# Second feed-forward product of a transformer block by seven half-size block products, a quarter of the depth at a time, two of them kept in PSUM

## The chip, the cores and the metric

The program runs on one core of a Trainium2 chip. The metric is the time on the device in microseconds (us), from the start of the execution to its end. The kernel before took 733.24 us, the median of three runs (732.91 to 734.58).

## The reference

One block of an encoder over 512 rows of width 1024: two attention branches, a gated mix, a layer norm, a feed-forward layer with a squared ReLU, and a second layer norm. Weights and rows are float32. What follows the two branches is

```python
x = layer_norm(DEEPNORM_ALPHA * x + mix, ln1_g[l], ln1_b[l])

h = jnp.square(jax.nn.relu(jnp.einsum("bsd,df->bsf", x, w_ff1[l])))
ff = jnp.einsum("bsf,fd->bsd", h, w_ff2[l])
x = layer_norm(DEEPNORM_ALPHA * x + ff, ln2_g[l], ln2_b[l])
```

Here `w_ff1` is 1024 x 4096 and `w_ff2` is 4096 x 1024. The first product contracts over 1024, the second over 4096; both have 512 rows.

## The kernel before

**Products of split operands.** TensorE multiplies in a reduced float32 format, so each operand is kept as two parts: a rounded one (h) and the rest (l). `split` (L82 to L87) makes them: ScalarE's cast (L84) writes h, VectorE's subtraction (L85) writes l. One product of a 128x128 block by a 128x512 block is then three matmuls, h by h, h by l and l by h: `tmm` where the weights are the stationary operand (L184 to L186), `smm` where the rows are (L189 to L191).

**The feed-forward layer** runs in two halves of the hidden width (`hf`, 2048 columns each). In a half:

- First product: eight calls of `t_pair`, each with two PSUM banks of hidden units (128 units by 512 rows), 8 depth blocks x 3 matmuls per bank. `evac_h` takes a bank out: maximum with zero on VectorE (L850), the square on VectorE (L851), then a split. The results stay in SBUF, transposed, units in partitions, and are the stationary operand of the second product.
- Second product: for each half of the output columns (`nh`) one `s_group`, four banks (128 rows by 512 columns), 16 depth blocks x 3 matmuls per bank. VectorE adds a finished bank to the residual rows `x1`. In the very last group the fourth row block is cut into two pieces of 256 columns (`cut_last`), each row block's second layer norm follows its bank, and the rows are stored.

The very first pair of banks is cut into columns 0 to 255 and 256 to 511, so that it can begin before the last row block of the first layer norm is transposed.

**Weights.** `w` is one stream of chunks, 128 x 1024 (512 KB) each. `chunk` and `prefetch` load a chunk on SP's queue (L126) into one of three `raw` buffers and split it, double-width, into one of three `wh` and `wl` buffers. A cast thus waits until TensorE has read the buffer's old chunk.

**The order.** A tile scheduler takes the program's order, with few exceptions, as the order of each engine's queue, and puts a wait on each instruction that needs another engine's result or a free buffer. In the first half, the first layer norm's scaling of the residual rows (`affine`, L742 and L748, four instructions for each of four row blocks) stands behind the pairs 1 to 4.

**SBUF and PSUM.** SBUF tiles of 128 x 512 come from rings named X (16), G (16) and V (24); PSUM has eight banks, "mm" (4), "st" (3) and "o" (1), taken in turn by `mm_bank`.

## Time and profile before

| | |
|---|---|
| median of three runs | 733.24 us |
| the profiled execution | 734.16 us, of it 732.3 us are the span |
| mean granted TensorE clock | 0.996 |
| TensorE / VectorE / ScalarE busy | 98% / 60% / 41% of the span |
| first product, first half (from its second pair on) | 385.6 to 461.7 us |
| second product, first half | 461.7 to 548.8 us |
| first product, second half | 548.8 to 635.8 us |
| second product, second half | 635.8 to 723.6 us |
| last addition starts; span ends | 723.75; 732.3 us |

In the rows, PE is TensorE, PEld its weight loads, DVE VectorE, ACT ScalarE, POOL GpSimd, SP the engine whose queue holds most DMA issues. Times are us from the span's start. In a timeline row come start, duration, engine, line, operation, output <- input, shape; in brackets the idle time of that engine before the instruction and what ended it. Instructions of one engine overlap at their ends: the distance between two starts is shorter than one duration. In a table by stretch each engine has its busy time and, in parentheses, the instructions. Of a busy share over the whole span, ask first in which stretch it arises.

### The profile page before, as it was taken

What the parts mean: (1) busy time and instruction counts of PE and PEld (TensorE: products, weight loads), DVE (VectorE), ACT (ScalarE), POOL (GpSimd) and SP (SyncE); (2) the same over time, 40 slices, a digit from 0 to 9 for tenths busy, and PEclk for the clock granted to TensorE, in tenths of its full rate; (3) what the DMA queues carried; (4) which work ended last, traced back from release to release, by engine and by line L of the source; (5) the groups of instructions that cost most, each with busy time, mean ns of one, the idle gap of its engine ahead of it and who ended that gap; (6) DMA issues with size and microseconds to landing.
All of it is one profiled execution on the core that took longest, in us unless ns stands there. A gap on an engine that the chain in (4) does not pass through costs nothing.

```text
span 732.3 us, 9147 instructions
## 1 busy us (share of the span) xinstructions
PE 720.5 (98%) x3391; PEld 602.2 (82%) x3391; DVE 437.6 (60%) x780; ACT 298.3 (41%) x506; POOL 100.5 (14%) x107
## 2 busy tenths in 40 slices
PE   9999999999999999999999999999999999999995
PEld 7888888888888888888898888888888888888884
DVE  6667668766667666745877885423235655523555
ACT  5556566645667755324353322212112332322200
POOL 2022266730121120051000000000000000000001
PEclk9999999999999999999999999999999999999998
DMA  8554223331431213464113223232232223322302
GB/s 295 199 155 134 74 84 91 99 117 58 128 102 60 85 59 115 151 225 171 58 59 115 87 86 116 87 115 87 91 111 87 96 83 110 102 100 87 115 30 86
DMA packets 27596, 78.86 MB, mean 108 GB/s; under 512 B 4640, under 2 KB 5408, under 8 KB 27552
## 3 DMA queue, kind: packets, MB, share of 16 engines
q1 hardware_dynamic: 26688, 77.17, 32.2%
q10 hardware_dynamic: 864, 1.11, 0.4%
q8 instruction: 26, 0.43, 0.2%
q14 instruction: 18, 0.15, 0.1%
HBM read 71.45 MB, written 2.10 MB: 100 GB/s over the span
## 4 chain that ended last, share of the span: by engine, by line
PE 95%; ACT 2%; DVE 2%; DMA 0%; issue 0%; DVEq 0%
PE mm L184 13%; PE mm L186 13%; PE mm L185 13%; PE mm L189 7%; PE mm L191 7%; PE mm L190 7%; PE st L191 4%; PE st L190 4%; PE st L189 4%; PE st L186 3%; PE st L185 3%; PE st L184 3%; PE o L191 2%; PE o L190 1%; PE o L189 1%; PE st L278 1%
## 5 line engine op out<-in xcount | busy, mean ns | idle before, releaser
L85 DVE TENSOR_TENSOR wl<-raw,wh 128x1024 fp32r<-128x1024 f32 (+1 forms) x116 | 141.7, 1222 | 120.8 <-ACT wh L84 120.8
L84 ACT CAST wh<-raw 128x1024 fp32r<-128x1024 f32 (+1 forms) x116 | 120.2, 1036 | 195.9 <-PE st L191 65.8
L184 PE MATMUL mm<-X,wh 128*128 128x512 f32 x256 | 103.2, 403 | 0.0
L186 PE MATMUL mm<-X,wl 128*128 128x512 f32 x256 | 99.9, 390 | 0.0
L185 PE MATMUL mm<-X,wh 128*128 128x512 f32 x256 | 99.8, 390 | 0.0
L186 PEld LDWEIGHTS mm<-X,wl 128*128 128x128 f32 x256 | 48.0, 188 | 10.6
L184 PEld LDWEIGHTS mm<-X,wh 128*128 128x128 f32 x256 | 48.1, 188 | 8.8
L185 PEld LDWEIGHTS mm<-X,wh 128*128 128x128 f32 x256 | 48.2, 188 | 8.6
L773 POOL TENSOR_SCALAR s<-s 128x1 f32<-128x1 f32 x1 | 0.4, 412 | 388.2 <-DVE s L757 388.2
L189 PE MATMUL mm<-wh,X 128*128 128x512 f32 (+1 forms) x128 | 51.0, 400 | 0.6 <-ACT wh L84 0.6
L287 ACT ACTIVATE e<-e,s 128x128 f32<-128x128 f32 (+3 forms) x64 | 36.0, 563 | 35.4 <-DVE s L285 34.6
L190 PE MATMUL mm<-wl,X 128*128 128x512 f32 (+1 forms) x128 | 50.3, 393 | 0.0
L191 PE MATMUL mm<-wh,X 128*128 128x512 f32 (+1 forms) x128 | 50.3, 393 | 0.0
L184 PE MATMUL mm<-x1t_h,wh 128*128 128x512 f32 x128 | 49.8, 389 | 0.0
L185 PE MATMUL mm<-x1t_l,wh 128*128 128x512 f32 x128 | 49.8, 389 | 0.0
L186 PE MATMUL mm<-x1t_h,wl 128*128 128x512 f32 x128 | 49.8, 389 | 0.0
L380 POOL TENSOR_SCALAR e<-e,s 128x128 f32<-128x128 f32 (+3 forms) x32 | 36.8, 1149 | 65.9 <-DVE s L289 62.0
L84 ACT CAST V<-lt 128x512 fp32r<-128x512 f32 x24 | 14.9, 620 | 62.8 <-DVE lt L851 62.8
L186 PE MATMUL st<-x1t_h,wl 128*128 128x512 f32 (+1 forms) x104 | 38.8, 373 | 0.0
L185 PE MATMUL st<-x1t_l,wh 128*128 128x512 f32 (+1 forms) x104 | 38.7, 373 | 0.0
L184 PE MATMUL st<-x1t_h,wh 128*128 128x512 f32 (+1 forms) x104 | 38.5, 374 | 0.0
L566 POOL TENSOR_SCALAR e<-e,s 128x128 f32<-128x128 f32 (+3 forms) x16 | 19.1, 1196 | 93.2 <-DVE s L565 67.8
(259 smaller groups left out, 1532.8 us busy)
## 6 DMA issues: line engine op xcount, KB each, us to landing
raw<-in_w_dram SPq DMA_DIRECT2D x118, 512.0 KB
q<-q SPq DMA_DIRECT2D x32, 128.0 KB
G<-in_relb_dram SPq DMA_DIRECT2D x8, 256.0 KB
x<-in_x_dram SPq DMA_DIRECT2D x4, 512.0 KB
...
```

Source lines behind the costliest of these rows:

```text
L84: A.copy(out=h, in_=src)
L85: i = (eng or V).tensor_tensor(out=l, in0=src, in1=h.bitcast(F32), op=ALU.subtract)
L184: T.matmul(ps, lw_h, rh, start=first, stop=False)
L185: T.matmul(ps, lw_h, rl, start=False, stop=False)
L186: T.matmul(ps, lw_l, rh, start=False, stop=last)
L189: T.matmul(ps, ah, w_h, start=first, stop=False)
L190: T.matmul(ps, ah, w_l, start=False, stop=False)
L191: T.matmul(ps, al, w_h, start=False, stop=last)
L278: T.matmul(ps[:, :n], q2[:, sl], k1[:, :n], start=False, stop=True)
L287: A.activation(e[:, :n], e[:, :n], AF.Exp, bias=nm, scale=-1.0, accum_out=sums)
L380: G.tensor_scalar(ex[:, :n], ex[:, :n], r, None, op0=ALU.mult)
L566: G.tensor_scalar(e2[:, :n], e2[:, :n], r2l, None, op0=ALU.mult)
```

## The change

The second product becomes Strassen's scheme (Winograd's form), a quarter of the hidden width (1024) at a time. In a quarter the hidden rows A (512 x 1024) and the weights B (1024 x 1024) are seen as 2 x 2 blocks, and seven products of sums of blocks replace eight products of blocks. Of A, rows 0 to 255 and 256 to 511 and the two halves of the quarter's depth are the blocks; of B, the halves of the depth and of the columns. A block product is 2 row blocks x 4 depth blocks x 3 matmuls.

- **Quarters.** The layer runs in four quarters: four pairs of the first product (the pair i makes depth block i of A's left and of its right half), then the seven products. In quarter 0 the first layer norm's scaling stands behind pair 1 (two row blocks) and pair 2 (two).
- **Left operands.** `square` has the ReLU on ScalarE and the square on VectorE. `first` and `second` form the sums of A's blocks at half width (256 rows) and split them.
- **Right operands.** Each depth block of `w2` is loaded as four 128 x 512 tiles on SP's queue. `prepare(n, i)` splits the operand of product n, and forms differences in place ahead of later ones. The lower right block is overwritten and loaded a second time for product 3, behind product 5's split. Splits are single-width.
- **Products.** The order is 1, 6, 2, 7, 5, 4, 3. Products 7 and 5 (`W`, `Z`) stay in four "mm" banks over all four quarters; the others go through the four remaining banks. The sum of products 1 and 6 over the quarters stands in SBUF (`U`), and products 1, 2, 4 and 3 are added to the residual rows `x1` in each quarter.
- **The last quarter.** `U`, `W` and `Z` are added to the residual rows, and products 7, 5, 4, 3 run by row block, so that layer norms and stores follow row block by row block (2, 0, 1, 3). The last product is cut into two pieces of 256 columns, as before.

The core of the diff:

```diff
-    def s_group(act_h, act_l, evac, before=None, nk=4, tail=1, cut_last=False, ahead=2):
+    def s_group(act_h, act_l, evac, before=None, nk=4, tail=1, ahead=2):
 
         jobs = [(s, 0, S) for s in range(NT)]
-        if cut_last:
-            jobs[-1:] = [(NT - 1, 0, S // 2), (NT - 1, S // 2, S)]
...
-    rotation[:] = ["o", "st", "st", "st", "mm", "mm", "mm", "mm"]
+    rotation[:] = ["o", "st", "st", "st"]
...
-        def evac_h(ps):
-            r = tmp_tile()
-            V.tensor_scalar(r, ps, 0.0, None, op0=ALU.max)
-            V.tensor_tensor(out=r, in0=r, in1=r, op=ALU.mult)
-            big_h = vt if len(hh) < 12 else (lambda: xt(FR))
-            h, l = big_h(), big_h()
-            split(r, h, l)
-            hh.append(h)
-            hl.append(l)
...
+    lnc1 = [[xt() for _ in range(2)] for _ in range(2)]
+    load_ln(ln1_g, ln1_b, lnc1)
...
+    U = [late.tile([P, S], F32, name=f"u{b}") for b in range(2)]
+    touched = set()
+
+    def add_to(s, nh, ps, lo=0, hi=S):
+        y = x1[s][:, nh * S + lo:nh * S + hi]
+        if (s, nh) in touched:
+            V.tensor_tensor(out=y, in0=y, in1=ps, op=ALU.add)
+        else:
+            V.scalar_tensor_tensor(out=y, in0=y, scalar=ALPHA, in1=ps, op0=ALU.mult, op1=ALU.add)
+            touched.add((s, nh))
...
+    def sub(out, a, b):
+        V.tensor_tensor(out=out, in0=a, in1=b, op=ALU.subtract)
...
+    LEFT = {1: "A11", 2: "A12", 3: "S4", 4: "A22", 5: "S1", 6: "S2", 7: "S3"}
+    lo_rows, hi_rows = slice(0, 256), slice(256, S)
...
+            a11 = self.halves(vt)
+            self.ops[1] = [(vt(), vt()) for _ in range(4)]
+            s2 = self.halves(vt)
+            self.ops[6] = [(vt(), vt()) for _ in range(4)]
+            s3 = self.halves(lambda: late.tile([P, S], FR, tag="s3", bufs=4, name=name("s3")))
...
+        def halves(self, make):
+
+            two = [(make(), make()) for _ in range(2)]
+            return [tuple(t[:, 256 * j:256 * (j + 1)] for t in pair)
+                    for pair in two for j in range(2)]
...
+        def square(self, ps):
+            t = tmp_tile()
+            A.activation(t, ps, AF.Relu)
+            V.tensor_tensor(out=t, in0=t, in1=t, op=ALU.mult)
+            return t
+
+        def first(self, i):
+            def f(ps):
+                t = self.t0 = self.square(ps)
+                sub(t[:, hi_rows], t[:, lo_rows], t[:, hi_rows])
+                split(t[:, lo_rows], *self.a["A11", i])
+                split(t[:, hi_rows], *self.a["S3", i])
+            return f
...
+        def second(self, i):
+            def f(ps):
+                t, t0 = self.square(ps), self.t0
+                s2 = tmp_tile()[:, lo_rows]
+                sub(s2, t[:, hi_rows], t0[:, hi_rows])
+                for left, right in (("A12", "A22"), ("S4", "S1")):
+                    h, l = gt(FR), gt(FR)
+                    split(t, h, l)
+                    self.a[left, i] = h[:, lo_rows], l[:, lo_rows]
+                    self.a[right, i] = h[:, hi_rows], l[:, hi_rows]
+                    if left == "A12":
+                        split(s2, *self.a["S2", i])
+                        sub(t[:, lo_rows], t[:, lo_rows], s2)
+                        V.tensor_tensor(out=t[:, hi_rows], in0=s2, in1=t0[:, lo_rows], op=ALU.add)
+            return f
...
+        def loads(self, i):
+            self.raw[i] = [self.load(i, r, c) for r, c in ((0, 0), (0, 1), (1, 1), (1, 0))]
+
+        def prepare(self, n, i, parts=None):
+            b11, b12, b22, b21 = self.raw[i]
+            src = {1: b11, 6: b22, 2: b21, 7: b12, 5: b11, 4: b22, 3: b11}[n]
+            if n == 6:
+                sub(b22, b22, b11)
+            self.ops[n][i] = self.ops[n][i] or parts or (vt(), vt())
+            split(src, *self.ops[n][i])
+            if n == 1:
+                sub(b11, b12, b11)
+                sub(b12, b22, b12)
+            if n == 6:
+                sub(b22, b21, b22)
+            if n == 5:
+                self.load(i, 1, 1, b11)
+
+        def run(self, n, ps, blocks=(0, 1), first=True, stop=True, cuts=((0, S),)):
+            jobs = [(b, lo, hi) for b in blocks for lo, hi in cuts]
+            order = [(j, i) for i in range(4) for j in jobs] if n == 1 else                 [(j, i) for j in jobs for i in range(4)]
+            for (b, lo, hi), i in order:
+                ah, al = (t[:, b * P:(b + 1) * P] for t in self.a[LEFT[n], i])
+                wh, wl = (t[:, lo:hi] for t in self.ops[n][i])
+                smm(ps[b][:, lo:hi], ah, al, wh, wl, first and i == 0, stop and i == 3)
...
+    for q in range(4):
+        qt, last = Quarter(q), q == 3
+        for i in range(4):
+            for n in ((0,), (1, 2), (3,), ())[i] if q else (i,):
+                qt.loads(n)
...
-                for _ in t_pair(*zip(*(x1t(k) for k in range(KD))), [evac_h, evac_h]):
+                for _ in t_pair(*zip(*(x1t(k) for k in range(KD))), evacs):
...
+            if q == 0 and i in (1, 2):
+                for s in (2, 3) if i == 1 else (0, 1):
+                    affine(s, *norm.pop(s), *lnc1)
+            for n, k in ((), ((1, 0),), ((1, 1), (6, 0)), ((1, 2), (1, 3), (6, 1)))[i]:
+                qt.prepare(n, k)
+
+        def prepare(n, which=range(4), parts=None):
+            for i in which:
+                qt.prepare(n, i, parts and [t[:, i, :] for t in parts])
...
+        if last:
+            t, p3h, p3l = (late.tile([P, 4, S], dt, tag="x1t", bufs=4, name=name("x1t"))
+                           for dt in (F32, FR, FR))
+            lnc = [[t[:, 2 * i + j, :] for j in range(2)] for i in range(2)]
+            load_ln(ln2_g, ln2_b, lnc)
...
+        if q == 0:
+            W, Z = ([bank("mm") for _ in range(2)] for _ in range(2))
+        ends = dict(first=q == 0, stop=last)
+        X = bank_pair()
+        qt.run(1, X)
+        prepare(6, (2, 3))
+        for b in range(2):
+            if q == 0:
+                A.copy(out=U[b], in_=X[b])
             else:
+                V.tensor_tensor(out=U[b], in0=U[b], in1=X[b], op=ALU.add)
+            add_to(b, 0, X[b])
+        prepare(2)
+        X = bank_pair()
+        qt.run(6, X)
+        prepare(7)
+        for b in range(2):
+            V.tensor_tensor(out=U[b], in0=U[b], in1=X[b], op=ALU.add)
+        X = bank_pair()
+        qt.run(2, X)
+        prepare(5)
+        for b in range(2):
+            add_to(b, 0, X[b])
             if last:
+                row_stats(b, 0)
+        if not last:
+            qt.run(7, W, **ends)
+            prepare(4)
+            qt.run(5, Z, **ends)
+            prepare(3)
+            X = bank_pair()
+            qt.run(4, X)
+            prefetch(next_chunk[0] + 4, next_chunk[0] + 2)
+            for b in range(2):
+                add_to(b + 2, 0, X[b])
+            X = bank_pair()
+            qt.run(3, X)
+            for b in range(2):
+                add_to(b, 1, X[b])
+            continue
+
+        prepare(4)
+        prepare(3, parts=(p3h, p3l))
+        for b in range(2):
+            for s, nh in ((b + 2, 1), (b + 2, 0), (b, 1)):
+                add_to(s, nh, U[b])
+        qt.run(7, W, (0,), **ends)
+        add_to(2, 1, W[0])
+        add_to(2, 0, W[0])
+        qt.run(5, Z, (0,), **ends)
+        add_to(2, 1, Z[0])
+        row_stats(2, 1)
+        X, Y = bank_pair(), bank_pair()
+        qt.run(4, X, (0,))
+        add_to(2, 0, X[0])
+        row_stats(2, 0)
+        layer_norm(2, *lnc, store_row(2))
+        add_to(0, 1, Z[0])
+        qt.run(3, Y, (0,))
+        add_to(0, 1, Y[0])
+        row_stats(0, 1)
+        layer_norm(0, *lnc, store_row(0))
+        qt.run(5, Z, (1,), **ends)
+        add_to(1, 1, Z[1])
+        add_to(3, 1, Z[1])
+        qt.run(3, Y, (1,))
+        add_to(1, 1, Y[1])
+        row_stats(1, 1)
+        layer_norm(1, *lnc, store_row(1))
+        qt.run(7, W, (1,), **ends)
+        add_to(3, 0, W[1])
+        add_to(3, 1, W[1])
+        row_stats(3, 1)
+        for lo, hi in ((0, 256), (256, S)):
+            qt.run(4, X, (1,), cuts=((lo, hi),))
+            add_to(3, 0, X[1][:, lo:hi], lo, hi)
+            row_stats(3, 0, lo, hi)
+        layer_norm_last(3, *lnc, store_row(3))
...
-    for hf in range(2):
-        for fp in range(8):
-            c = 2048 * hf + 256 * fp
-            parts.append(t_form(w_ff1[:, c:c + P], w_ff1[:, c + P:c + 2 * P]))
-        for nh in range(2):
-            parts.append(s_form(w_ff2[2048 * hf:2048 * hf + 2048, 512 * nh:512 * nh + 512]))
+    for q in range(4):
+        for i in range(4):
+            c = 1024 * q + P * i
+            parts.append(t_form(w_ff1[:, c:c + P], w_ff1[:, c + 512:c + 512 + P]))
...
+        "w2": a["w_ff2"][0].reshape(4, 2, 4, P, D).transpose(0, 2, 1, 3, 4),
```

How the order moves. The names are the pools' tiles with running numbers: `lt` hidden units before their split, `o`, `st` and `mm` PSUM banks, `wl`, `wh` and `raw` weight chunks of the first product, `x1_` the residual rows, `bn` statistics. In the new kernel X holds a quarter's raw weight blocks and V and G operands; L866 there is `sub`, L897 the square, L896 the ReLU, L853 `add_to`, L85 still the split.

VectorE, the end of the first product. Before, the last pair of the first half:

```order
L850 TENSOR_SCALAR lt982_4422<-mm981_4397 128x512
L851 TENSOR_TENSOR lt982_4422<-lt982_4422 128x512
L85 TENSOR_TENSOR wl990_4438<-raw985_4429,wh989_4437 128x1024
L85 TENSOR_TENSOR X984_4426<-lt982_4422,X983_4425 128x512
L850 TENSOR_SCALAR lt992_4466<-mm991_4441 128x512
L851 TENSOR_TENSOR lt992_4466<-lt992_4466 128x512
L85 TENSOR_TENSOR X994_4470<-lt992_4466,X993_4469 128x512
L85 TENSOR_TENSOR wl1005_4512<-raw988_4435,wh1004_4511 128x1024
L850 TENSOR_SCALAR lt996_4498<-mm995_4473 128x512
L851 TENSOR_TENSOR lt996_4498<-lt996_4498 128x512
L85 TENSOR_TENSOR wl1008_4542<-raw1003_4509,wh1007_4541 128x1024
L85 TENSOR_TENSOR X998_4502<-lt996_4498,X997_4501 128x512
```

The same place at the end of quarter 1's last pair, in the new kernel:

```order
L897 TENSOR_TENSOR lt1143_5016<-lt1143_5016 128x512
L866 TENSOR_TENSOR X1115_4843<-X1116_4845,X1115_4843 128x512
L866 TENSOR_TENSOR lt1144_5019<-lt1143_5016,lt1141_4983 128x256
L85 TENSOR_TENSOR G1146_5022<-lt1143_5016,G1145_5021 128x512
L85 TENSOR_TENSOR V1064_4636<-lt1144_5019,V1063_4635 128x256
L866 TENSOR_TENSOR lt1143_5016<-lt1143_5016,lt1144_5019 128x256
L921 TENSOR_TENSOR lt1143_5016<-lt1144_5019,lt1141_4983 128x256
L866 TENSOR_TENSOR X1116_4845<-X1117_4847,X1116_4845 128x512
L866 TENSOR_TENSOR X1094_4740<-X1094_4740,X1092_4736 128x512
L85 TENSOR_TENSOR G1148_5030<-lt1143_5016,G1147_5029 128x512
L866 TENSOR_TENSOR X1098_4748<-X1098_4748,X1096_4744 128x512
L85 TENSOR_TENSOR V1068_4640<-X1094_4740,V1067_4639 128x512
```

The maximum is gone from VectorE; between the square and the next pieces of the pair stand differences and splits of the right operands.

ScalarE at the same place, before:

```order
L84 CAST X983_4425<-lt982_4422 128x512
L84 CAST X993_4469<-lt992_4466 128x512
L84 CAST wh1004_4511<-raw988_4435 128x1024
L84 CAST wh1007_4541<-raw1003_4509 128x1024
L84 CAST X997_4501<-lt996_4498 128x512
L84 CAST wh1010_4571<-raw1006_4539 128x1024
L84 CAST wh1013_4601<-raw1009_4569 128x1024
L84 CAST wh1016_4631<-raw1012_4599 128x1024
```

ScalarE in the new kernel, at the end of quarter 1's last pair:

```order
L84 CAST wh1199_5301<-raw1137_4952 128x1024
L84 CAST V1059_4631<-X1115_4843 128x512
L84 CAST V1051_4623<-lt1141_4983 128x256
L84 CAST s31075_4647<-lt1141_4983 128x256
L84 CAST wh1235_5371<-raw1197_5297 128x1024
L896 ACTIVATE lt1143_5016<-st1142_4991 128x512
L84 CAST G1145_5021<-lt1143_5016 128x512
L84 CAST V1063_4635<-lt1144_5019 128x256
```

The last pair's first instruction on ScalarE is now the ReLU, with a weight cast (for a chunk of the next first product) directly ahead of it; before, it was the cast of the squared units.

VectorE at the end of the program, before:

```order
L888 TENSOR_TENSOR x1_2_3208<-x1_2_3208,mm1209_5876 128x512
L894 BN_STATS bn1197_5854<-x1_2_3208 128x6
L734 BN_AGGR s1234_6129<-bn1197_5854 128x2
L742 SCALAR_TENSOR_TENSOR x1_2_3208<-x1_2_3208,s1234_6129,G807_3405 128x512
L747 RECIPROCAL s1236_6131<-s1235_6130 128x1
L742 SCALAR_TENSOR_TENSOR x1_2_3208<-x1_2_3208,s1234_6129,G808_3406 128x512
L748 SCALAR_TENSOR_TENSOR x1_2_3208<-x1_2_3208,s1236_6131,G809_3407 128x512
L748 SCALAR_TENSOR_TENSOR x1_2_3208<-x1_2_3208,s1236_6131,G810_3408 128x512
L888 TENSOR_TENSOR x1_3_3209<-x1_3_3209,mm1210_5877 128x256
L894 BN_STATS bn1198_5863<-x1_3_3209 128x6
L888 TENSOR_TENSOR x1_3_3209<-x1_3_3209,o1211_5878 128x256
L894 BN_STATS bn1198_5863<-x1_3_3209 128x6
```

VectorE at the same place in the new kernel:

```order
L853 TENSOR_TENSOR x1_3_3213<-x1_3_3213,mm992_4328 128x512
L736 SCALAR_TENSOR_TENSOR x1_0_3210<-x1_0_3210,s1504_6726,x1t1453_6465 128x512
L741 RECIPROCAL s1506_6728<-s1505_6727 128x1
L736 SCALAR_TENSOR_TENSOR x1_0_3210<-x1_0_3210,s1504_6726,x1t1453_6465 128x512
L742 SCALAR_TENSOR_TENSOR x1_0_3210<-x1_0_3210,s1506_6728,x1t1453_6465 128x512 x2
L863 BN_STATS bn1487_6620<-x1_1_3211 128x6
L853 TENSOR_TENSOR x1_3_3213<-x1_3_3213,mm992_4328 128x512
L728 BN_AGGR s1507_6766<-bn1487_6620 128x2
L853 TENSOR_TENSOR x1_3_3213<-x1_3_3213,st1498_6682 128x256
L736 SCALAR_TENSOR_TENSOR x1_1_3211<-x1_1_3211,s1507_6766,x1t1453_6465 128x512
L741 RECIPROCAL s1509_6768<-s1508_6767 128x1
```

In the new kernel a row half of `x1` gets several additions, of `mm` (products 7 and 5) and `st` banks, where it got one, and additions of row block 3 stand between the instructions of row block 0's and 1's layer norms.

## Rows read from the trace of the kernel before

**Rows 1.** Part 1 of the page: busy us, share of the span, instructions
```profile
PE 720.5 (98%) x3391; PEld 602.2 (82%) x3391; DVE 437.6 (60%) x780; ACT 298.3 (41%) x506; POOL 100.5 (14%) x107
```

**Rows 2.** Part 2, the span in forty slices: VectorE's tenths, TensorE's granted clock
```profile
DVE  6667668766667666745877885423235655523555
...
PEclk9999999999999999999999999999999999999998
```

**Rows 3.** Part 4, the chain that ended last, by engine
```profile
PE 95%; ACT 2%; DVE 2%; DMA 0%; issue 0%; DVEq 0%
```

**Rows 4.** Busy time by stretch: first, second, first, second product; clock, DMA share, GB/s
```profile
385.60:461.70 76.10, 76.10 (x339) 63.10 (x339) 57.64 (x74) 23.71 (x30) 0.00 (x0) 1.00 0.30 97
461.70:548.80 87.10, 87.10 (x386) 72.09 (x386) 25.95 (x26) 17.50 (x17) 0.00 (x0) 1.00 0.31 103
548.80:635.80 87.00, 87.00 (x385) 72.06 (x384) 50.16 (x62) 26.16 (x31) 0.00 (x0) 1.00 0.27 91
635.80:723.60 87.80, 87.80 (x433) 74.51 (x431) 37.67 (x54) 16.33 (x20) 0.00 (x0) 1.00 0.27 90
```

**Rows 5.** Timeline of TensorE, end of the first product: start, duration
```profile
457.66 0.39 PE L184 MATMUL mm<-x1t_h,wh 128*128 128x512 f32 x1
...
461.74 0.39 PE L189 MATMUL o<-wh,V 128*128 128x512 f32 x1
```

**Rows 6.** Timeline at the end: the last matmuls and the last addition
```profile
723.31 0.28 PE L190 MATMUL o<-wl,X 128*128 128x256 f32 x1
...
723.43 0.28 PE L191 MATMUL o<-wh,X 128*128 128x256 f32 x1
723.75 0.42 DVE L888 TENSOR_TENSOR x<-x,o 128x256 f32<-128x256 f32 x1 [1.90 <-PE o L191]
```

**Rows 7.** Timeline of VectorE in the first product of the first half
```profile
429.30 0.69 DVE L850 TENSOR_SCALAR lt<-st 128x512 f32<-128x512 f32 x1 [0.59 <-PE st L186]
430.03 0.69 DVE L851 TENSOR_TENSOR lt<-lt 128x512 f32<-128x512 f32 x1
430.63 1.22 DVE L85 TENSOR_TENSOR wl<-raw,wh 128x1024 fp32r<-128x1024 f32 x1
431.77 0.68 DVE L85 TENSOR_TENSOR V<-lt,V 128x512 fp32r<-128x512 f32 x1
432.37 0.74 DVE L742 SCALAR_TENSOR_TENSOR x<-x,ln,G 128x512 f32<-128x512 f32 x1
433.15 0.75 DVE L748 SCALAR_TENSOR_TENSOR x<-x,ln,G 128x512 f32<-128x512 f32 x1
433.82 0.75 DVE L742 SCALAR_TENSOR_TENSOR x<-x,ln,G 128x512 f32<-128x512 f32 x1
```

**Rows 8.** Timeline of VectorE, half-width instructions near the end
```profile
720.97 0.42 DVE L888 TENSOR_TENSOR x<-x,mm 128x256 f32<-128x256 f32 x1
721.42 0.43 DVE L894 BATCH_NORM_STATS2 bn<-x 128x6 f32<-128x256 f32 x1
```

**Rows 9.** Timeline of ScalarE where the second product begins
```profile
461.76 1.05 ACT L84 CAST wh<-raw 128x1024 fp32r<-128x1024 f32 x1 [1.67 <-PE mm L185]
```

**Rows 10.** Groups of ScalarE by form: a 128x512 activation out of PSUM
```profile
L484 ACT ACTIVATE G<-mm 128x512 f32<-128x512 f32 x8 | 4.8, 600 | 5.4 <-PE mm L186 5.3
```

**Rows 11.** Timeline at the second bank pair: VectorE and ScalarE
```profile
383.45 0.69 DVE L850 TENSOR_SCALAR lt<-o 128x512 f32<-128x512 f32 x1 [2.51 <-PE o L186]
...
386.12 1.05 ACT L84 CAST wh<-raw 128x1024 fp32r<-128x1024 f32 x1
```

**Rows 12.** Busy time and clock behind the last matmul
```profile
726.60:732.00 5.40, 0.00 (x0) 0.00 (x0) 1.69 (x3) 0.00 (x0) 1.25 (x2) 0.50 0.29 99
```

**Rows 13.** Timeline of TensorE at the start of the run
```profile
5.97 0.63 PE L190 MATMUL mm<-wl,X 128*128 128x512 f32 x1
6.39 0.63 PE L191 MATMUL mm<-wh,X 128*128 128x512 f32 x1
```

More of the change, by code (lines that the diff above doesn't have):

```diff
@@ L390, in attn_a @@
             yield
-    cos_t = const.tile([P, S], F32, name="cos_t")
-    sin_t = const.tile([P, S], F32, name="sin_t")
-    other = [const.tile([P, S], F32, name=f"other{i}") for i in range(2)]
+    cos_t = tables.tile([P, S], F32, name="cos_t")
+    sin_t = tables.tile([P, S], F32, name="sin_t")
+    other = [tables.tile([P, S], F32, name=f"other{i}") for i in range(2)]
     lam = const.tile([P, 1], F32, name="lam")
@@ L693, in block_kernel @@
     x1 = [late.tile([P, D], F32, name=f"x1_{s}") for s in range(NT)]
-    x1t_h = [late.tile([P, 4, S], FR, name=f"x1t_h{i}") for i in range(2)]
-    x1t_l = [late.tile([P, 4, S], FR, name=f"x1t_l{i}") for i in range(2)]
+    x1t_h, x1t_l = ([late.tile([P, 4, S], FR, tag="x1t", bufs=4, name=name("x1t"))
+                     for _ in range(2)] for _ in range(2))
     gb1 = late.tile([P, 2, KD], F32, name="gb1")
@@ L706, in block_kernel, with tmp_tile @@
         nc.sync.dma_start(out=gb1[:, j, :], in_=src)
-    def tmp_tile():
-        return late.tile([P, S], F32, tag="lt", bufs=4, name=name("lt"))
+    def tmp_tile(dt=F32):
+        return late.tile([P, S], dt, tag="lt", bufs=4, name=name("lt"))
     for _ in branch(1, ob_h, ob_l):
         pass
-    lnc1 = [[gt() for _ in range(2)] for _ in range(2)]
-    load_ln(ln1_g, ln1_b, lnc1)
-    lnc = [[gt() for _ in range(2)] for _ in range(2)]
-    load_ln(ln2_g, ln2_b, lnc)
     stats, norm = {}, {}
@@ new lines, in row_stats @@
+    def row_stats(s, nh, lo=0, hi=S):
+        width = S if s < NT - 1 else 256
+        if s not in stats:
+            stats[s] = sm.tile([P, D // width, 6], F32, tag=f"bn{width}", bufs=4, name=name("bn"))
+        for c in range(nh * S + lo, nh * S + hi, width):
+            V.bn_stats(out=stats[s][:, c // width, :], in_=x1[s][:, c:c + width])
+    def sub(out, a, b):
+        V.tensor_tensor(out=out, in0=a, in1=b, op=ALU.subtract)
+    LEFT = {1: "A11", 2: "A12", 3: "S4", 4: "A22", 5: "S1", 6: "S2", 7: "S3"}
@@ new lines, in first_pair @@
+    def first_pair(evacs):
+        ch = [chunk() for _ in range(2)]
+        ps2 = [mm_bank() for _ in range(2)]
+        for lo, hi in ((0, 256), (256, 512)):
+            for j in range(2):
+                if (lo, j) == (0, 1):
+                    x1_transposed(NT - 1)
+                for k in range(KD):
+                    wh, wl = ch[k // 4]
+                    off = (k % 4) * 256 + j * 128
+                    sl = slice(off % 512, off % 512 + 128)
+                    tmm(ps2[j][:, lo:hi], wh[off // 512][:, sl], wl[off // 512][:, sl],
+                        *x1t(k, lo, hi), k == 0, k == KD - 1)
+        for j in range(2):
+            evacs[j](ps2[j])
@@ new lines, in store_row, with store, bank_pair @@
+    def store_row(s):
+        def store(cols):
+            q = A if cols.start in (S, 832) else nc.sync
+            q.dma_start(out=out[s * P:(s + 1) * P, cols], in_=x1[s][:, cols])
+        return store
+    def bank_pair():
+        return [mm_bank() for _ in range(2)]
+    for q in range(4):
[3 more added lines that the diff above has]
+                qt.loads(n)
+            evacs = [qt.first(i), qt.second(i)]
+            if q == 0 and i == 0:
+                first_pair(evacs)
@@ L911, in s_form, with _weight_stream @@
+        layer_norm_last(3, *lnc, store_row(3))
+def _weight_stream(w_in, w_branch_a, w_branch_b, w_out, w_ff1):
     def s_form(m):
@@ L934, in _weight_stream @@
         parts.append(s_form(w_out[:, 512 * nh:512 * nh + 512]))
[L935 to L940 removed]
+    for q in range(4):
+        for i in range(4):
+            c = 1024 * q + P * i
+            parts.append(t_form(w_ff1[:, c:c + P], w_ff1[:, c + 512:c + 512 + P]))
     return np.concatenate(parts, 0)
```

69 lines of the change are left out of this document (17 added, 52 removed).

## The prediction

> **What bounds the kernel now.** Read the page's busy times first [rows 1]: TensorE is busy 98% of the span, VectorE 60%. That is an average, so the forty slices come next [rows 2]: the clock granted to TensorE stays in the 9s to the last slice, and VectorE falls from 6 to 8 tenths in the first half to 2 to 5 in the second, where the feed-forward layer lies. The chain that ended last is TensorE for 95% [rows 3]. The stage table cuts the feed-forward layer into its four stretches [rows 4]: in the two stretches of the second product (461.7 to 548.8 and 635.8 to 723.6) TensorE has no idle time and full clock, VectorE works 26.0 and 37.7 of 87 us. So a matmul taken out there shortens the run by its own spacing, as long as nobody makes TensorE wait. Over the whole layer VectorE is busy 171.4 of 338.0 us (the four stretches of rows 4): there is room on average, and the question is whether the room lies where the new work falls.
>
> **Part 1, what goes.** Consecutive matmuls of 512 columns start 0.2267 us apart (18 of them from 457.66 to 461.74 [rows 5]), those of 256 columns 0.12 apart [rows 6]. The second product was 720 wide and 96 narrow matmuls, and is 660 and 24 (built order: 3391 TensorE instructions become 3259, so the change does what it says). Removed: 60 x 0.2267 + 72 x 0.12 = **22.2 us**, if nothing waits. It is the whole possible gain.
>
> **Part 2, what VectorE gets.** Per quarter and depth block: eleven full-width operations for the right-hand operands (seven splits, four differences) where the old order had two double-width splits' worth; seven half-width and four full-width for the left ones; the maximum moves to ScalarE. Per quarter also 10 to 12 additions out of PSUM. Over the layer VectorE goes from 216 instructions and 171.4 busy us to some 480. I count them in slots, the distance between starts in a full queue [rows 7]: 0.605 for a full-width two-operand instruction (430.03 to 430.63, 431.77 to 432.37), 0.73 if the next reads its result (429.30 to 430.03), 1.14 for a double-width split (430.63 to 431.77), 0.67 for one with a scalar (433.15 to 433.82), 0.78 if dependent. Half-width was seen only dependent, 0.45 (720.97 to 721.42 [rows 8]); that is 0.28 under the dependent full one, so I take 0.34. Sums below use the independent slots and the built order, and so lean low.
>
> **Part 3, quarters 1 and 2.** T is the end of the quarter's last first-product matmul. In the new ScalarE order a 1024-wide weight cast stands directly before the last relu, and its buffer comes free only with that matmul: the trace of before has the same cast start at 461.76, 0.02 after the last matmul's slot, and take 1.05 [rows 9]. The relu follows (about 0.60, as the 128x512 activation out of PSUM [rows 10]), so VectorE's last squaring starts at T+1.6. From there to the split that product 7's second matmul needs stand 30 instructions: 24 x 0.605 + 4 x 0.34 + 2 x 1.14 = 18.2. The split starts at T+19.8 and is done at T+20.5. TensorE needs it after 72 matmuls of products 1, 6 and 2 and one more: T+16.8 with the semaphore. Wait: **3.7 us in each of the two quarters**, in pieces of about 1 us. Behind it VectorE has some 20 instructions against 96 matmuls (21.8 us), and in the next first product 30.7 us of slots against 43.5, so nothing is carried over.
>
> **Part 4, quarter 0.** Here the sixteen first-layer-norm operations (0.67 each, 10.7 us) lie in the same queue. The old order had them too, but with half the other work. The second bank pair's first squaring can start at 393.0: the first relu at 383.45, the weight cast at 386.12 [rows 11], then 15 VectorE instructions of the new order with their casts. From it to the last split of product 2's operand stand 84 instructions: 39 x 0.605 + 18 x 0.67 + 21 x 0.34 + 6 x 1.14 = 49.6, and I add 2.0 for four places where the queue waits for a cast whose buffer TensorE frees. The split is done at 445.4, product 2 ends four matmuls later at 446.3. Without waits the second pair begins at 461.74 - 7 x 10.88 = 385.6, three pairs end at 418.2, products 1, 6, 2 and one matmul at 434.8. Wait: **11.5 us**.
>
> **Part 5, quarter 3.** No next quarter hides its queue, and it holds three layer norms, the sums in U added to six half rows, and both remaining accumulators. From the squaring at T+0.8 (no weight cast stands in front) to the last addition stand 90 instructions: 62 x 0.605 + 14 x 0.67 + 8 x 0.34 and six small ones (1.1) = 50.7, so the addition starts at T+51.5. TensorE without waits would end its 168 matmuls' worth at T+38.2 and let it start 0.3 later, as 723.75 follows 723.43 [rows 6]. Overhang: **13.0 us**. TensorE is idle in it, no matmul can shorten it. What follows the last addition is unchanged: 723.75 to the span's end at 732.3.
>
> **Part 6, the rest.** DMA: the lower right block is fetched twice, 4.2 MB more over 340 us that carried 90 to 103 GB/s at a share of about 0.3 [rows 4]; on SP's queue those loads stand before later weight chunks and wait for VectorE's product-5 splits, but the chunks behind them are due 20 us later. I take 0; if a chunk is late it costs its own 2 to 3 us. The relu on ScalarE: 16.3 to 26.2 of 87 us busy there [rows 4], 160 more instructions of at most 0.6 us, fed ahead of VectorE: 0.
>
> **The sum.** -22.2 + 11.5 + 3.7 + 3.7 + 13.0 = **+9.7 us**. The profiled execution took 734.2 (span 732.3), so 743.9; the median is 0.9 lower, so 743.0.
>
> **The clock.** In quarter 0 TensorE stands still for some 5 us (424 to 429, before the third block's operand of product 1). At the end of before the granted clock is 0.50 from 726.6 on, with the last matmul at 723.43 [rows 6, 12]; at the start of the run wide matmuls are 0.42 apart [rows 13], in the feed-forward layer 0.23 [rows 5]. [...] I take 0 for it: VectorE's queue, not TensorE, sets the time until 446, and of the 48 matmuls that TensorE has from 429 on, 20 at 0.42 and 28 at 0.23 make 15 of those 17 us; if it stays down longer, that is rival (b). [...]
>
> **Rivals.**
> (a) VectorE keeps up, and the run is not slower. TensorE stays the bound, the waits of parts 3 to 5 shrink. Price: with none of them 711; the sign turns where they total 22.2 instead of 31.9. These rest on 49.6 + 2 x 18.2 + 50.7 = 137 us of slots, so it takes slots 7% shorter, 0.56 in place of 0.605 for a full operand. For it: half-width slots are inferred. Against it: every independent full-width pair in rows 7 reads 0.60 to 0.61, and VectorE's order is fixed in the program. I put 722 on it.
> (b) The clock falls and stays down over part of the waiting stretches. [...] For it: the 5 us idle in quarter 0. Against it: the granted clock stays in the 9s to the last slice [rows 2].
> [...]
>
> **How the numbers follow.** The forecast gets 0.70: its own range is 737 (cast waits of quarters 0 to 2 gone, some slots shorter) to 750 (a third of the in-place pairs at 0.73 and 0.78: 5 us; a late chunk: 2). Rival (a) 0.13, between 711 and 733; rival (b) 0.17, 744 to 753. Leaving out most of (a) and the top of (b) gives 734.5 to 751. A measurement of this kernel tells 0.2%, 1.5 us, from no change: faster 0.11, same 0.04, slower 0.85, the last from the forecast, (b) and the edge of (a).
>
> **What would show it.** In the profile after, VectorE must be near 9 tenths in the slices of each quarter's first half of products and in the last stretch; the TensorE waits must name VectorE's split line as releaser, longest in the first quarter's product 1; the last matmul must end about 11 us before the last addition; the matmuls of the first product in quarters 1 to 3 must stay 0.2267 apart. Wrong would be: a last addition within 1 us of the last matmul (part 5 falls), no waits at product 6 and 2 (part 3), waits that name a DMA (part 6), or matmuls 0.42 apart after quarter 0 (rival b).

## The result and the profile after

The changed kernel takes 743.66 us (median of 4 runs, 742.20 to 744.27), the kernel before 733.66 in the same comparison: 1.0133 times the time (95% interval 1.0113 to 1.0153), 10.0 us slower. The prediction was 743.0 us (734.5 to 751.0).

The page of the kernel after, parts 1, 2 and 4 (compare [rows 1 to 3]):

```profile
PE 709.8 (96%) x3259; PEld 583.1 (79%) x3259; DVE 546.9 (74%) x1046; ACT 361.9 (49%) x666; POOL 100.5 (14%) x107
...
DVE  6567578765678656747779996389946798288998
...
PEclk9999999999999999999999989999999999999996
...
PE 73%; DVE 20%; ACT 4%; issue 2%; DMA 1%; DVEq 0%; ACTq 0%
```

VectorE is not full on average (74%), but reaches 9 tenths in four places: three slices in quarter 0, two from the end of quarter 1's first product into its products, one in quarter 2's products, two near the end, with 8 tenths around them. There the chain of waits runs over VectorE, 20% where it was 2%.

The same layer by stretches, cut at the first matmul of each product and at the last addition (compare [rows 4]; columns as there):

```profile
377.70:419.00 41.30, 41.26 (x214) 34.94 (x212) 35.22 (x63) 21.85 (x39) 0.00 (x0) 1.00 0.39 132
419.00:468.00 49.00, 41.76 (x170) 32.35 (x168) 39.25 (x66) 19.05 (x34) 0.00 (x0) 0.93 0.46 150
468.00:511.50 43.50, 43.50 (x193) 36.04 (x192) 30.91 (x53) 21.04 (x36) 0.00 (x0) 1.00 0.22 73
511.50:553.90 42.40, 40.34 (x170) 31.08 (x169) 33.30 (x56) 16.31 (x29) 0.00 (x0) 1.00 0.44 149
...
597.40:639.70 42.30, 40.25 (x169) 31.07 (x168) 33.25 (x56) 16.29 (x29) 0.00 (x0) 1.00 0.44 150
...
683.20:734.20 51.00, 41.47 (x181) 33.00 (x179) 50.87 (x94) 15.66 (x30) 0.00 (x0) 0.93 0.18 60
```

168 wide matmuls take 168 x 0.2267 = 38.1 us. The products of quarters 0, 1 and 2 take 49.0, 42.4 and 42.3, so TensorE waits 10.9, 4.2 and 4.2 us; the first products (43.5) wait for nothing. In the last stretch VectorE is busy for 50.87 of 51.0 us. (Exact starts are used below: 418.96, 511.52, 597.39 and 683.24 for the first matmul of the products, 734.19 for the last addition.)

### The profile page after: what moved, and what is told of

The parts are those of the page before. It is cut to its first block, busy times and chain, and to the rows that moved or that the text cites. A ratio compares the mean times of both kernels' runs of the same rounds, so it can differ in the third digit from the quotient of the medians.

```text
span 742.2 us, 9457 instructions
## 1 busy us (share of the span) xinstructions
PE 709.8 (96%) x3259; PEld 583.1 (79%) x3259; DVE 546.9 (74%) x1046; ACT 361.9 (49%) x666; POOL 100.5 (14%) x107
## 4 chain that ended last, share of the span: by engine, by line
PE 73%; DVE 20%; ACT 4%; issue 2%; DMA 1%; DVEq 0%; ACTq 0%
PE mm L184 9%; PE mm L186 9%; PE mm L185 9%; DVE V L85 5%; PE st L184 4%; PE st L185 4%; PE st L186 4%; PE mm L190 4%; PE mm L191 4%; PE mm L189 4%; DVE X L866 3%; PE st L190 2%; PE st L191 2%; PE st L189 2%; DVE G L85 1%
## 5 line engine op out<-in xcount | busy, mean ns | idle before, releaser
L85 DVE TENSOR_TENSOR wl<-raw,wh 128x1024 fp32r<-128x1024 f32 (+1 forms) x86 | 105.0, 1221 | 27.1 <-ACT wh L84 27.1
L84 ACT CAST V<-X 128x512 fp32r<-128x512 f32 x108 | 61.6, 618 | 40.3 <-DMA X<-in_w_dram 25.1
L186 PE MATMUL st<-x1t,wl 128*128 128x512 f32 (+1 forms) x200 | 76.1, 381 | 0.0
L185 PE MATMUL st<-x1t,wh 128*128 128x512 f32 (+1 forms) x200 | 76.1, 381 | 0.0
L184 PE MATMUL st<-x1t,wh 128*128 128x512 f32 (+1 forms) x200 | 75.9, 381 | 0.0
L85 DVE TENSOR_TENSOR V<-X,V 128x512 fp32r<-128x512 f32 x108 | 70.9, 680 | 5.0 <-ACT V L84 5.0
L186 PEld LDWEIGHTS st<-x1t,wl 128*128 128x128 f32 x200 | 37.6, 188 | 7.6 <-DVE wl L85 0.5
L185 PEld LDWEIGHTS st<-x1t,wh 128*128 128x128 f32 x200 | 37.6, 188 | 7.2
L184 PEld LDWEIGHTS st<-x1t,wh 128*128 128x128 f32 x200 | 37.5, 188 | 7.0
L866 DVE TENSOR_TENSOR X<-X,X 128x512 f32<-128x512 f32 x64 | 42.3, 680 | 0.1
L189 PE MATMUL mm<-wh,X 128*128 128x512 f32 x96 | 39.0, 409 | 0.7 <-ACT wh L84 0.7
L190 PE MATMUL mm<-wl,X 128*128 128x512 f32 x96 | 38.4, 400 | 0.0
```

What stands on the lines that cost most here:

```text
L84: A.copy(out=h, in_=src)
L85: i = (eng or V).tensor_tensor(out=l, in0=src, in1=h.bitcast(F32), op=ALU.subtract)
L184: T.matmul(ps, lw_h, rh, start=first, stop=False)
L185: T.matmul(ps, lw_h, rl, start=False, stop=False)
L186: T.matmul(ps, lw_l, rh, start=False, stop=last)
L189: T.matmul(ps, ah, w_h, start=first, stop=False)
```

## Experiments

E1 to E12 are edits of the changed kernel, which is "changed" below. Times are medians; ratios are to the kernel before. "Excess" is a stretch of products less its 38.1 us.

### E3: is it the clock in quarter 0?

```diff
             for m, ((b, lo, hi), i) in enumerate(order):
+                if n == 1 and self.q == 0 and m == 6:
+                    for _ in range(23):
+                        T.matmul(W[0], x1t(0)[0][:, 0:P], x1t(0)[0], start=True, stop=True)
```

> Changed kernel with 23 more matmuls of 512 columns (5.2 us) into an unused bank, in quarter 0 where TensorE stands still for 5.5 us, so that it does not rest. Theory (VectorE sets the time there, the lower clock behind the rest costs nothing): 743.7 us, within 0.5. Rival (the clock costs): the matmuls from 429 to 433 us, now 0.43 apart, come 0.23 apart and the run is 2 to 3 us shorter.

Changed, VectorE's split and the timeline of TensorE at the halt: 5.3 us idle for that split, then matmuls 0.43 apart to 433.25, where they were 0.23 apart ahead of it; the granted clock is 0.50 from 428.97 to 433.25:

```profile
428.23 0.68 DVE L85 TENSOR_TENSOR V<-X,V 128x512 fp32r<-128x512 f32 x1
...
423.27 0.39 PE L191 MATMUL st<-V,V 128*128 128x512 f32 x1
428.97 0.80 PE L190 MATMUL o<-V,V 128*128 128x512 f32 x1 [5.31 <-DVE V L85]
429.56 0.63 PE L191 MATMUL o<-V,V 128*128 128x512 f32 x1
429.99 0.63 PE L190 MATMUL st<-V,V 128*128 128x512 f32 x1
```

E3, the same place with the 23 matmuls in the halt, and what follows:

```profile
420.34 5.38 PE L954 MATMUL mm<-x1t 128*128 128x512 f32 x23
425.55 0.39 PE L189 MATMUL st<-V,V 128*128 128x512 f32 x1
...
433.86 0.90 PE L189 MATMUL st<-V,V 128*128 128x512 f32 x2 [1.26 <-ACT V L84]
435.02 0.80 PE L190 MATMUL st<-V,V 128*128 128x512 f32 x1 [0.26 <-DVE V L85]
435.61 0.63 PE L191 MATMUL st<-V,V 128*128 128x512 f32 x1
436.04 0.63 PE L189 MATMUL st<-V,V 128*128 128x512 f32 x1
```

743.31 us, ratio 1.0127 (1.0110 to 1.0144): no change. Behind the filled halt the matmuls are 0.23 apart (425.55, 425.78, 426.00), and the run gets nothing for it: they meet new waits for VectorE and ScalarE's casts a few us later (1.26 us at 433.86). Quarter 0's products take 49.1 us, as in changed (49.0), though they hold 5.2 us more of TensorE's work and the granted clock is 0.97 there, not 0.93. So the clock rival falls as the cause. E3 alone does not take the lower clock out wholly, since the matmuls are 0.43 apart again later, behind those shorter waits (435.61 to 437.32); E6 below has a clock of 1.00 in this stretch, and 5.7 us of waits stay.

### E6, E1: the first layer norm in quarter 0's queue

E6 keeps the work on VectorE and moves half of it to where VectorE waits:

```diff
-                    affine(s, *norm.pop(s), *lnc1)
+                    affine(s, *norm[s], *lnc1, halves=(0,))
 ...
             for b in range(2):
                 add_to(b + 2, 0, X[b])
+            if q == 0:
+                lnc1 = ln1_half(1)
+                for s in range(NT):
+                    affine(s, *norm.pop(s), *lnc1, halves=(1,))
```

> Changed kernel, with the first layer norm's scaling of columns 512 to 1023 (8 of the 16 operations) moved to the end of quarter 0, where VectorE waits, on VectorE still; gain and bias of those columns are loaded there. Theory: 8 x 0.665 = 5.3 us leave the full queue ahead of product 6 in quarter 0, its TensorE excess falls from 10.9 to some 5.5: 738.4 us, the other quarters unchanged. Rival (the clock or the loads set quarter 0): 742 to 744. With GpSimd out of it, VectorE's distances between starts stay 0.60.

737.60 us, ratio 1.0056 (1.0036 to 1.0076), 6.1 less than changed. Quarter 0's products fall from 49.0 to 43.8 us, and the clock there is 1.00, not 0.93:

```profile
417.80:461.60 43.80, 40.24 (x169) 31.01 (x168) 38.55 (x65) 18.31 (x33) 0.00 (x0) 1.00 0.46 156
```

E1 takes all sixteen off VectorE (eight instructions on ScalarE and sixteen on GpSimd in their place, a pair earlier in the order):

```diff
+                        A.activation(y, y, AF.Identity, bias=nmr, scale=rs)
+                        G.tensor_tensor(out=y, in0=y, in1=lnc1[0][j], op=ALU.mult)
+                        G.tensor_tensor(out=y, in0=y, in1=lnc1[1][j], op=ALU.add)
```

> Changed kernel, with the sixteen scalings of the first layer norm in quarter 0 taken off VectorE (ScalarE normalises, GpSimd multiplies and adds, 16 operations of some 1.74 us as in the rows of L615). Theory (VectorE's queue sets quarter 0): it loses 16 x 0.665 = 10.6 us ahead of product 6; quarter 0's TensorE excess falls from 10.9 to the 4.2 of quarters 1 and 2, so about 7 us less than the changed kernel: 736.5 us. Rival (the clock, or loads of the operands, set quarter 0): little change, 742 to 744. Rival (GpSimd's operations slow VectorE's): VectorE's distance between starts rises above 0.60, gain under 4 us.

742.03 us, ratio 1.0111 (1.0094 to 1.0128): a miss by 5.5 us, on the side of its second rival. The products of quarter 0 did what the theory said (41.2 us, excess 3.1), but the first product ahead of them lost 6 us. VectorE in E1, while GpSimd works (first the VectorE rows, then GpSimd's last):

```profile
386.78 1.40 DVE L866 TENSOR_TENSOR lt<-lt 128x256 f32<-128x256 f32 x1
388.11 2.31 DVE L85 TENSOR_TENSOR wl<-raw,wh 128x1024 fp32r<-128x1024 f32 x1
390.34 1.51 DVE L85 TENSOR_TENSOR V<-lt,V 128x256 fp32r<-128x256 f32 x1
...
397.14 0.41 DVE L866 TENSOR_TENSOR lt<-lt,lt 128x256 f32<-128x256 f32 x1
...
394.51 1.62 POOL L999 TENSOR_TENSOR x<-x,X 128x512 f32<-128x512 f32 x1
```

A half-width instruction took 1.4 to 1.5 us until GpSimd was done (396.13), and 0.41 after it. A weight split (`wl`) took 2.31 us there, 1.21 in changed (528.67), and one came late: TensorE waited 3.1 us for it in the first product. Behind the wait the matmuls are 0.43 apart (from 405.68 on), 0.23 ahead of it (400.02 to 400.93), and the granted clock of the whole stretch (377.9 to 425.1) is 0.96:

```profile
405.09 0.80 PE L186 MATMUL o<-x1t,wl 128*128 128x512 f32 x1 [3.06 <-DVE wl L85]
405.68 0.63 PE L184 MATMUL o<-x1t,wh 128*128 128x512 f32 x1
```

### E7: GpSimd again, in the last quarter

```diff
-            V.tensor_tensor(out=y, in0=y, in1=ps, op=ALU.add)
+            eng.tensor_tensor(out=y, in0=y, in1=ps, op=ALU.add)
 ...
-                add_to(s, nh, U[b])
+                add_to(s, nh, U[b], eng=G)
```

> Changed kernel, in the last quarter four additions of U to the rows moved from VectorE to GpSimd, all in SBUF. By what the run with the scalings on GpSimd showed (VectorE's instructions take 1.4 to 2.3 us beside GpSimd's, some 0.9 us lost per GpSimd operation), VectorE saves 4 x 0.6 and loses 4 x 0.9: 745 us, no gain. Rival (GpSimd is a free engine): 2.4 us less, 741.3 us.

744.94 us, ratio 1.0159 (1.0145 to 1.0173). VectorE and GpSimd in E7:

```profile
698.68 1.77 DVE L855 SCALAR_TENSOR_TENSOR x<-x,u 128x512 f32<-128x512 f32 x1
700.38 1.75 DVE L85 TENSOR_TENSOR V<-X,V 128x512 fp32r<-128x512 f32 x1
702.05 1.78 DVE L855 SCALAR_TENSOR_TENSOR x<-x,u 128x512 f32<-128x512 f32 x1
703.75 0.68 DVE L85 TENSOR_TENSOR V<-X,V 128x512 fp32r<-128x512 f32 x1
...
696.66 6.62 POOL L853 TENSOR_TENSOR x<-x,u 128x512 f32<-128x512 f32 x4 [360.34 <-DVE u L1025]
```

Four GpSimd operations in 6.62 us, and VectorE starts one instruction per GpSimd operation (700.38 and 702.05, so every 1.7 us, not 0.60): some 1.1 us lost for 0.6 saved.

### E2, E4, E5: quarters 1 and 2

E2 loads and prepares products 1 and 6 one pair earlier in quarters 1 to 3:

```diff
-            for n in ((0,), (1, 2), (3,), ())[i] if q else (i,):
+            for n in ((0, 1), (2, 3), (), ())[i] if q else (i,):
 ...
+                         ((), ((1, 0), (1, 1), (6, 0)), ((1, 2), (6, 1), (1, 3), (6, 2)), ())[i]):
 ...
-        prepare(6, (2, 3))
+        prepare(6, (3,) if q else (2, 3))
```

> Changed kernel, with the loads and preparations of products 1 and 6 one pair earlier in quarters 1 to 3. Theory: eight instructions leave VectorE's queue between the last square and product 7's operand, the TensorE excess of 4.2 us in quarters 1 and 2 falls to under 1 us each, and in quarter 3 some 4 us of VectorE's work moves into its gaps before 673 us: 743.7 - 3.5 - 3.5 - 4 = 732.7 us. Rival (the waits come from ScalarE's late ReLU, not from VectorE's count): quarters 1 and 2 keep 3 to 4 us each, 739 us or more.

731.94 us, ratio 0.9976 (0.9966 to 0.9985). Quarters 1 and 2 take 38.7 us each for their products (quarter 1 below), and the last stretch 47.4:

```profile
511.20:549.90 38.70, 38.65 (x169) 31.28 (x168) 29.70 (x50) 15.55 (x28) 0.00 (x0) 1.00 0.48 163
```

The instructions are the same; those for products 1 and 6 stand a pair (10.9 us) earlier in the order, their loads and casts with them, and eight leave VectorE's queue between the last square and product 7's operand. That gives back 11.7 us.

E4 holds the next quarter's first weight splits back behind product 5's operands (the pair then asks for no chunk ahead; a pinned `prefetch` follows `prepare(5)`):

```diff
+        if not last:
+            pinned[0] = 2
+            prefetch(next_chunk[0] + 2, next_chunk[0] + 2)
+            pinned[0] = False
```

> Changed kernel, with the split of the next quarter's first weight chunks (cast and subtraction) held back behind product 5's operands in quarters 0 to 2, so that no cast stands before the last ReLU and no double-width subtraction in VectorE's critical stretch. Theory: quarters 1 and 2 lose 1.05 + 2 x 1.14 = 3.3 of their 4.2 us each, quarter 0 about 1.1, quarter 3 nothing: 736.0 us. Rival (the cast before the ReLU is hidden): quarters 1 and 2 lose at most 2.3 each, 738 us; rival (late splits make the next quarter's first matmuls wait): no gain.

737.89 us, ratio 1.0051 (1.0033 to 1.0068): 5.8 us less than changed where 7.7 were expected. Quarter 0 gave 2.0 (1.1 expected), quarters 1 and 2 1.8 and 1.7, not 3.3. The waits that stay, 2.5 us in quarter 1, lie at products 6 and 2, ahead of the two double-width subtractions (528.67 and 530.41 in changed), so their 2.3 us could not all be had; and the cast had held the last ReLU for 0.7 us only (it starts 0.97 us behind the last first-product matmul in changed, 0.26 in E4).

E5 squares on ScalarE:

```diff
             A.activation(t, ps, AF.Relu)
-            V.tensor_tensor(out=t, in0=t, in1=t, op=ALU.mult)
+            A.activation(t, t, AF.Square)
```

> Changed kernel, with the square of the hidden units on ScalarE too (a second pass of some 0.6 us), so that VectorE has 8 full-width operations less per quarter. Theory (VectorE's count sets the time): quarter 0 loses the four squares that lie behind 403 us where the queue is full, 4 x 0.6 = 2.4 us; quarters 1 and 2 have 25 instructions in place of 30 between the last unit block and product 7's operand, less 0.6 for the later start, 2.4 us each of their 4.2; the last quarter loses the 3 to 4 squares that lie in its full queue, 2 us: 743.7 - 9.2 = 734.5 us. Rival (ScalarE becomes late instead): no gain, 742 us or more.

734.98 us, ratio 1.0018 (1.0007 to 1.0029), as expected: quarter 0's products 46.4 us, quarter 1's 40.4, the last stretch 49.65 in place of 50.95. ScalarE has more work and VectorE less, and the time falls by 8.7 us: it was not ScalarE that held.

### E9, E12: the last quarter

E9 computes the last quarter plainly (`plain_quarter`; the sums in W, Z and U are finished in quarter 2):

```diff
-        ends = dict(first=q == 0, stop=last)
+        ends = dict(first=q == 0, stop=q == 2)
 ...
+        if q == 3:
+            plain_quarter(q)
+            break
```

> Changed kernel with the last quarter as a plain product (8 block products, 24 wide matmuls more, 5.4 us), the three sums of the earlier quarters added to the rows during its first product. Theory (the last quarter is set by VectorE's 90 instructions, not by TensorE): TensorE is the bound there again; the last addition starts 43.5 + 0.6 us after the last first-product matmul in place of 50.95, 6.9 us less: 736.8 us, though it has 5.4 us more matmuls. Rival (TensorE's matmuls set the last quarter, for example by the two column pieces that share a bank): 5.4 us more, 749 us; with the 2.5 us of the shared bank given back 746.5.

737.34 us, ratio 1.0048 (1.0031 to 1.0066). With 24 wide matmuls' worth of work more, the last stretch is 44.0 us and the last addition waits for the last matmul again:

```profile
683.20:727.20 44.00, 43.95 (x217) 37.21 (x215) 25.62 (x46) 4.19 (x9) 0.00 (x0) 1.00 0.14 48
...
727.19 0.42 DVE L853 TENSOR_TENSOR x<-x,o 128x256 f32<-128x256 f32 x1 [0.46 <-PE o L191]
```

E12 gives the two column pieces of the last product a bank each:

```diff
+        X2 = bank_pair()
 ...
-            qt.run(4, X, (1,), cuts=((lo, hi),))
+            qt.run(4, X if lo == 0 else X2, (1,), cuts=((lo, hi),))
```

> Changed kernel with the two column pieces of the last product in two PSUM banks, so that the second piece's matmuls need not wait for the addition of the first. Theory (VectorE sets the end, the wait of 7.9 us is hidden behind its queue): TensorE ends some 10 us earlier, the last addition starts as before, 743.7 us within 0.7. Rival (the shared bank makes the end late): 2.5 us less, 741.2 us.

743.15 us, ratio 1.0125 (1.0106 to 1.0144): no change, though TensorE's last matmul starts at 725.60, 8.9 us ahead of the last addition (734.52). The wait of 7.9 us is down to 1.15.

### E8: the second fetch

```diff
-            if n == 5:
+            if n == 5 and False:
                 self.load(i, 1, 1, b11)
```

> Changed kernel without the second fetch of the lower right weight block (16 loads of 256 KB; product 3 then multiplies what the buffer held, so its share of the result is another). Theory (the extra traffic is hidden): 743.7 us, within 0.7. Rival (SP's queue or the traffic makes something late): 2 us or more less.

742.76 us, ratio 1.0123 (1.0106 to 1.0141): 0.9 us less than changed, a little outside the expected 0.7 and far from the rival's 2; the intervals overlap. Quarter 0's products take 49.1 us again. No price of the traffic is seen; one of up to 1 us is not ruled out.

### E10, E11: together

E10 has the edits of E2, E4, E5, E6 and E9; E11 has those of E2, E4, E5, E6 and E12, with seven products in the last quarter.

> All edits that took VectorE's work out of the full stretches, together: preparations a pair earlier in quarters 1 to 3, the next quarter's weight splits behind product 5, the square on ScalarE, half of the first layer norm's scaling at the end of quarter 0, the last quarter plain. By the theory TensorE waits 2 to 3 us in quarter 0, 0.5 each in quarters 1 and 2, and not in the last: 733.8 - 22.2 + 5.4 + 3.5 = 720.5 us (719 to 724), faster than both kernels. Rival (the removed waits come back elsewhere, at ScalarE or the loads): 728 us or more.

> The same edits with the last quarter by seven products as in the changed kernel, its two last column pieces in banks of their own. By the theory VectorE still sets the last quarter: some 45.4 us from the last first-product matmul to the last addition in place of 44.0 in the plain one: 722 us (720 to 725). Rival (TensorE sets it, then seven products win): 38.5 us, 715 us.

E10: **718.92 us**, ratio 0.9803 (0.9790 to 0.9817). E11: 721.80 us, ratio 0.9842 (0.9828 to 0.9855). E10 beats the kernel before by 14.8 us. Its products of quarters 0 and 1 (quarter 2 takes 38.3 us) and its last quarter:

```profile
417.00:457.70 40.70, 39.30 (x169) 31.05 (x168) 36.73 (x60) 19.92 (x34) 0.00 (x0) 1.00 0.52 173
...
501.30:539.50 38.20, 38.20 (x169) 31.52 (x168) 28.02 (x46) 17.29 (x29) 0.00 (x0) 1.00 0.53 179
...
664.80:708.90 44.10, 44.03 (x217) 37.25 (x216) 25.06 (x45) 4.82 (x10) 0.00 (x0) 1.00 0.14 50
```

Only quarter 0 still waits, 2.6 us. Taken one at a time, the five edits of E10 gave 38.6 us, together 24.7: their gains overlap and must not be added up. In E11 the last stretch takes 46.2 us with VectorE busy for 46.0: in that place seven products cost more than eight, since they save TensorE 5.4 us and VectorE sets the end.

```profile
665.80:712.00 46.20, 38.83 (x181) 31.88 (x179) 46.00 (x86) 15.11 (x29) 0.00 (x0) 0.96 0.19 66
```

## Why the prediction was right, and where not

| term | predicted | measured |
|---|---|---|
| matmuls removed (part 1) | -22.2 | -22.2, by count |
| quarter 0 (part 4) | +11.5 | +11.3: 10.9 in the products, 0.4 in the first product |
| quarters 1 and 2 (part 3) | +3.7 each | +4.2 each |
| last quarter (part 5) | +13.0 | +12.5: 50.95 from the first matmul of the products to the last addition, less 38.2 and the 0.3 by which the addition follows |
| before the layer | 0 | +0.4 |
| sum to the last addition | +9.7 | +10.4: 734.19 against 723.75 [rows 6]; the terms add up to 10.4 |

The 0.4 us before the layer need not be the change's: the first product's stretch that begins at 377.7 us in changed begins anywhere between 375.6 and 377.9 in E1 to E12, with all but the same work ahead of it. Behind the last addition 0.5 us came back (8.0 us in place of 8.55), where the prediction had no change. The sum was right, and so were its terms; the runs show that its mechanism is VectorE's queue: E6 and E2 move instructions along it, with their loads and casts, take none away, and give 6.1 and 11.7 us; E5 moves some of it to ScalarE, and gives 8.7.

**The slots (part 2)** carried over. The half-width one, inferred as 0.34, is 0.34 in the trace of changed (406.02 to 406.36), a scaled one 0.66:

```profile
406.02 0.42 DVE L866 TENSOR_TENSOR lt<-lt 128x256 f32<-128x256 f32 x1
406.36 0.75 DVE L742 SCALAR_TENSOR_TENSOR x<-x,ln,X 128x512 f32<-128x512 f32 x1
407.02 0.74 DVE L736 SCALAR_TENSOR_TENSOR x<-x,ln,X 128x512 f32<-128x512 f32 x1
```

**Part 4** came out along its own path: product 2 of quarter 0 was put to end at 446.3, and its last matmul starts at 446.07, one slot ahead of that.

**Part 3** was right in size (3.7 us for 4.2) and only half right in its reason. The last square was put at T+1.6 (T is the last first-product matmul's end, here 511.52) behind the weight cast and the ReLU. It starts at 513.50, T+2.0, and the row before it is VectorE's own split of a right operand:

```profile
511.53 1.06 ACT L84 CAST wh<-raw 128x1024 fp32r<-128x1024 f32 x1
512.49 0.59 ACT L896 ACTIVATE lt<-st 128x512 f32<-128x512 f32 x1
...
512.90 0.68 DVE L85 TENSOR_TENSOR V<-X,V 128x512 fp32r<-128x512 f32 x1
513.50 0.68 DVE L897 TENSOR_TENSOR lt<-lt 128x512 f32<-128x512 f32 x1
...
531.55 0.68 DVE L85 TENSOR_TENSOR V<-X,V 128x512 fp32r<-128x512 f32 x1
...
525.80 0.50 PE L189 MATMUL st<-V,G 128*128 128x512 f32 x1 [0.97 <-DVE x L853]
```

From the square on the count held: product 7's split starts 18.05 us later (531.55), where 18.2 stood. The prediction had every wait end with a split, though. The longest one in quarters 1 and 2 (0.97 and 0.96 us, the last row) ends with an addition: product 2 can't start in a bank that VectorE has not yet emptied. It is the same queue, but what TensorE waits for there is a free bank, not an operand.

E4, which takes the cast and the weight splits out of this stretch, gave 1.8 of the 4.2 us; E2, which moves eight of VectorE's instructions out of it, gave 3.6.

**Part 5** had the price and not the picture. It said that TensorE would be done 11 us before the last addition, and named "a last addition within 1 us of the last matmul" as what would refute it. The trace shows just that, counted from the matmul's end: 0.64 us (1.05 from start to start):

```profile
730.21 0.37 DVE L853 TENSOR_TENSOR x<-x,st 128x256 f32<-128x256 f32 x1
730.49 0.74 DVE L736 SCALAR_TENSOR_TENSOR x<-x,s,x1t 128x512 f32<-128x512 f32 x1
730.63 0.58 PE L189 MATMUL st<-V,G 128*128 128x256 f32 x1 [7.91 <-DVE x L853]
...
731.23 0.73 DVE L736 SCALAR_TENSOR_TENSOR x<-x,s,x1t 128x512 f32<-128x512 f32 x1
731.88 1.41 DVE L742 SCALAR_TENSOR_TENSOR x<-x,s,x1t 128x512 f32<-128x512 f32 x2
733.14 0.41 PE L191 MATMUL st<-V,G 128*128 128x256 f32 x1
733.20 1.07 DVE L863 BATCH_NORM_STATS2 bn<-x 128x6 f32<-128x256 f32 x3
734.19 0.40 DVE L853 TENSOR_TENSOR x<-x,st 128x256 f32<-128x256 f32 x1
```

The second column piece lies in the bank of the first and waits 7.9 us for VectorE's addition from it. I had overlooked that both pieces share a bank (before, they were in "mm" and "o"). But VectorE goes from 730.21 to 734.19 without a gap and does not wait for that matmul, and E12 shows the wait to be free. Without that wait TensorE would still not have been done 11 us ahead, but 8.9 (E12). The sign was badly chosen: two engines that end together do not say which one held the other. The releaser in the brackets and the gapless queue do.

**The clock and rival (b).** The halt of 5 us, the fall to 0.43 us per matmul (granted clock 0.50) and its price of nothing came as forecast (E3), the halt before the third depth block's operand of product 1 as well: ahead of it lie the 12 matmuls of the first two depth blocks, two of the third that need no low part of the weights, and six of product 6. The 20 matmuls at 0.42 were an estimate; the trace has ten (428.97 to 433.25), 0.43 apart. In quarters 1 and 2, with waits of 0.1 to 1.0 us, the granted clock is 1.00. One sign of the lower clock after quarter 0 did come: in the last stretch the granted clock is 0.93, and behind the 7.9 us wait the narrow matmuls lie 0.21 apart, not 0.12. It cost nothing that the runs show: in E12 that stretch has 0.96 and takes the same 51.0 us. The 744 to 753 us of rival (b) were an estimate too: no run shows a price of the lower clock in the products; the one sign of it is E1's first product, where TensorE is busy for 43.3 us (377.9 to 425.1) in place of 41.3. **Rival (a)** needed slots 7% shorter; they were what rows 7 said. **Part 6** held: E8, no price of the fetch above 1 us; the 2 to 3 us for a late chunk were an estimate that no run shows (no wait of TensorE in changed names a DMA); ScalarE, 49% busy, is waited for by TensorE for 1.7 us in the whole run, no wait above 0.7.
